# Sums of weight quadrants by accumulating loads, a full-height key low half, and a new order of the seven products

## The chip, the cores and the metric

One core of one Trainium2 chip. The metric is device microseconds of one execution. The kernel before took 1159.19 us (median of 3 runs, 1158.86 to 1163.72).

## The reference, cut to what matters

One hybrid decoder layer on 512 tokens with 16 meta tokens ahead (T = 528), width 2048, in fp32. A pre-RMSNorm, one input projection of 8192 columns, two groups of eight heads (stick-breaking attention with 128-wide heads; differential attention with two 64-wide query/key components, QK-norm and partial rotary), SiLU gates, one output projection of 2048 by 2048, and the residual:

```python
proj = jnp.einsum('btd,de->bte', rms_norm(h, norm_w), w_in)      # 2048 -> 8192
z = q @ k.T / sqrt(128); tail = reverse_cumsum(log_keep) - log_keep
a = where(k_pos < q_pos, exp(log_sigmoid(z) + tail), 0)           # stick-breaking head
p = softmax(where(k_pos <= q_pos, s, -inf))                       # for components 0 and 1
w = p[0] - lam * p[1]                                             # differential head
mixed = concat([sb_o * silu(sb_g), rms_norm(df_o, subln_w) * (1 - lam_init) * silu(df_g)])
out = h + mixed @ w_out
```

## The kernel before, in words

Every fp32 matrix product is done as three fp32r matmuls: each operand is split into a high part (a copy by ScalarE) and a low part (what is left, a subtraction by VectorE), and hi x hi, hi x lo, lo x hi are accumulated (`split`, lines 124 to 126; `mm`, lines 259 to 264).

The projections go by *pairs* of 128-column blocks: 32 pairs of w_in (numbers 0 to 31) and 8 of w_out (32 to 39). Four pairs belong to a head number: differential keys and values, differential queries and gate, stick-breaking keys and values, stick-breaking queries and gate. Pairs 2 to 31 and 33 to 39 use Strassen's scheme in Winograd's form: the weights of a pair are four quadrants a11, a21, a22, a12, the activations are seven combinations (`ut`), and seven products take the place of eight (`proj_pair`, line 431; `STEPS`, line 56). Each product is 8 (or 7) x 3 matmuls of 264 or 256 columns. The weights' side needs the sums s1 to s4. They are made by GpSimd in place on the raw quadrants (`SUMS`, `w_sum`, line 183), in two halves of 128x512 each, and each half is then split (`w_prep`, line 204). `preps` (line 218) runs through the pairs' quadrants in the order of use and goes one step on after each product. Raw quadrants have four places (tag "wr"), the split halves four each (tags "wh" and "wl"), so that splits are at most two quadrants ahead of TensorE: a split takes the place of the one two products back.

The products land in banks of PSUM (tag "pj", four). ScalarE copies those that are used more than once (`copied`, line 445), GpSimd adds copies (`add`, line 450), VectorE adds the last term from the bank (`final`, line 461). The pairs of w_out add onto the residual's rows (`base`).

Attention of a head runs beside the projections of the next pairs: `Pace` deals it out in steps. A differential head (`diff_head`) goes through four blocks of 128 queries and two components. Per block and component TensorE makes the scores (line 783 with the keys' high half, 785 the mask on the diagonal in bf16, 786 with the keys' low half on the component's 64 partitions), VectorE takes the row maximum (788, 789), ScalarE the exponential (791); then VectorE combines both components (797 to 799). Scores lie in two PSUM places, exponentials of component 0 in tag "w1" (two places), of component 1 in tag "w3" (one). `diff_k` prepares the keys: norm, rope, high and low half; the high half is copied to the other component's partitions too, since the query tile holds its high part on the component's 64 partitions and its low part on the other 64.

Loads go by SyncE's queue (line 157 for weights), in the order of the code. The order of instructions on each engine is laid out by a planner that plays the program through with its own durations; `hp(offset=600)` raises the priority of weight preparation and evictions. It is fixed before the run: an engine waits at an instruction whose input is late, with all that stands behind it.

Of the kernel before, what the change touches and what calls it, by code (L numbers as in the profile page):

```python
# [18 lines left out]
P = 128  # L19
# [64 lines left out]
def build(nc, tc, ctx, hT, win, wout, wpl, xT, prm, cst, out):  # L84
# [24 lines left out]
    def w3_tile(name, dt=F32):  # L109
        return ww.tile([P, T], dt, tag="w3", name=name, bufs=1)  # L110
# [29 lines left out]
    LOADS = ("a21", "a22", "a11", "a12")  # L140
# [8 lines left out]
    def w_load(s, which):  # L149
        o = s - last_in - 1  # L150
        if which == "pl":
            t = (cos_t, sin_t)[s % 2][:, :2 * NP * P].rearrange("p (k n) -> p k n", n=P)
            nc.sync.dma_start(t, wpl[o])
        else:
            t = wp.tile([P, H, P], F32, tag="wr", name=f"wr{s}{which}", bufs=4)[:, :depth(s)]
            if s > 0:
                nc.sync.dma_start(t, (win[s] if o < 0 else wout[o])[QUADS.index(which)])
        raw[s, which] = t

    def w_loads(s):  # L160
        order = QUADS if s in (1, 2, last_in + 2) else LOADS
        for which in () if s == len(plan) else order if s <= last_in else (*order, "pl"):
            w_load(s, which)

    def w_split(src, nm, spare=None):
# [3 lines left out]
        else:  # L169
# [5 lines left out]

    SUMS = {"s1": ("a21", "a21", "a22", ALU.add), "s2": ("a11", "a21", "a11", ALU.subtract),
            "s3": ("a21", "a22", "a11", ALU.subtract), "s4": ("a12", "a12", "a11", ALU.subtract)}

    def w_sum(s, which, u):
        if which in SUMS:  # L180
            o, x, y, op = SUMS[which]
            with hp(offset=600):
                G.tensor_tensor(raw[s, o][:, u], raw[s, x][:, u], raw[s, y][:, u], op=op)  # L183

    def w_halves(s, u, *which):

        v = units(s)[u]
        if s == 0:
            ts = [raw[s, x][:, v] for x in which]
        else:  # L190
            t = wp.tile([P, 2, 4, P], F32, tag="wr", name=f"wr{s}{which[0]}{u}", bufs=4)
            ts = [t[:, j, :v.stop - v.start] for j in range(2)]
# [11 lines left out]
    def w_prep(s, which, summed=False):  # L204

        for v in units(s):
            if which == "pl":
                v = slice(0, 2 * NP)
            elif not summed:
                w_sum(s, which, v)  # L210
            src = raw[s, SUMS[which][0] if which in SUMS else which]
            with hp(offset=600):
                wops.setdefault((s, which), []).append((v, *w_split(src[:, v], f"w{s}{which}{v.start}")))
            if which == "pl":
                break

    def preps():


        for s in range(1, len(plan)):  # L220
            if s == last_in + 1:
                continue
            while (s, "a12") not in raw:
# [8 lines left out]
            for which in [x for _, x, _ in STEPS2] if s == 2 else ("a11", "s1", "s2", "s3", "a12", "pl", "a22", "s4"):  # L232
                if which == "pl" and s <= last_in:
                    continue
                if s == 2 and which == "s3":
                    for v in units(s):
                        w_sum(s, "s2", v)
                w_prep(s, which, s == 2 and which == "s2")
# [9 lines left out]
    def combine(k, x, y, n, E, L=V):  # L248
# [3 lines left out]
        E.tensor_tensor(xs[:, 0], xs[:, 1], xs[:, 0], op=ALU.subtract)  # L252
        E.tensor_tensor(xs[:, 1], ys[:, 1], xs[:, 1], op=ALU.subtract)
        split(*(t[:, T1:T3 + 1] for t in hl), xs)
        E.tensor_tensor(ys[:, 1], ys[:, 1], xs[:, 0], op=ALU.subtract)
        E.tensor_tensor(ys[:, 0], ys[:, 0], ys[:, 1], op=ALU.subtract)
# [30 lines left out]
    for pool, tag, n in ((ww, "st", 5), (ww, "w1", 2), (ww, "w3", 1), (ww, "sh", 1), (sp, "vh", 1), (sp, "vl", 1)):  # L287
# [143 lines left out]
    def proj_pair(s, dst, base=None):  # L431
# [10 lines left out]
        def copied(x):  # L442
            t = wp.tile([P, TH], F32, tag="ev", name=f"ev{s}_{x}", bufs=4)[:, :n]
# [4 lines left out]
        def add(x, y):  # L448
            with hp(offset=600):
                G.tensor_tensor(x, x, y, op=ALU.add)  # L450

        def final(x, e, c, y):
            if (s, "pl") in wops:
                while late:
                    late.pop()()
                yield from plain(bank(x), e, c, wops[s, "pl"], x == "g")
            if base:
                y = base(e, c)
            with hp(offset=600):
                for d, sl in dst(e, c):  # L460
                    V.tensor_tensor(d, bank(x)[:, sl], y[:, sl], op=ALU.add)
# [3 lines left out]
        m1 = m5 = m7 = u2 = None  # L465
        for x, which, b in STEPS if s > 2 else STEPS2:
            more = which == "s2"
            yield from product(bank(x), wops[s, which], b, not more, x in "agd" or s <= last_in, more)
            next(ahead, None)
            if which == "a11":  # L470
                m1 = copied(x)
                if base:
                    add(base(0, 0), m1)
            elif which == "s1":
                m5 = copied(x)
            elif which == "s3":
                m7 = copied(x)
                if u2 is not None:
                    add(m7, u2)
                if base:  # L480
                    add(base(1, 0), m7)
            elif which == "s2":
                u2 = copied(x)
                add(m5, u2)
                if m7 is not None:
                    add(m7, u2)
                if base:
# [573 lines left out]
```

## Time and profile before

| | us | share of the span |
|---|---|---|
| profiled execution, its own time | 1159.92 | |
| its span | 1158.1 | |
| TensorE matmul busy | 1085.9 | 94% |
| VectorE busy | 958.3 | 83% |
| GpSimd busy | 793.9 | 69% |
| ScalarE busy | 612.7 | 53% |
| mean granted TensorE clock | 0.971 | |

Matmuls are pipelined: the duration of one (0.28 us for 256 columns) is longer than the distance from its start to the next one's start, and the distance is what counts on TensorE. A row of a timeline gives start, duration, engine, line, operation, tiles, shapes and count; in brackets the idle time before it and who ended it.

### The profile page before, as it was taken

To read this page: it belongs to the slowest core of one execution; us is meant where nothing else is said; L and a number is where in the kernel's file an instruction comes from. 1 tells how busy PE (TensorE), PEld (TensorE's weight loads), DVE (VectorE), ACT (ScalarE), POOL (GpSimd) and SP (SyncE) were. 2 spreads that over 40 slices of the span, in tenths; PEclk is the share of its full clock that TensorE was granted. 3 is DMA by queue.
4 is the path that set the end of the run, shared out by engine and by line. 5 is a ranking of instruction groups with operands and counts; after the bars stand their busy time and mean duration, and the time that the engine had idled before them with its cause. 6 is when DMAs were issued, how large, how long until landed. Compare 5 with 4: busy or idle time off the path is not lost.

```text
span 1158.1 us, 22082 instructions
## 1 busy us (share of the span) xinstructions
PE 1085.9 (94%) x8247; PEld 1022.0 (88%) x8247; DVE 958.3 (83%) x1556; ACT 612.7 (53%) x1231; POOL 793.9 (69%) x597
## 2 busy tenths in 40 slices
PE   8899999899989998999899999999999997799998
PEld 7898899799979997999799988998999886799998
DVE  6879887898788878887888789878887898978886
ACT  9735554455445544654465446544654565444443
POOL 3566668767866687668765877687657746658886
PEclk9999999999998999899989999999899988899999
DMA  7212222222222222222222222222222233345441
GB/s 273 78 53 74 73 83 83 73 74 83 83 73 74 82 83 74 73 83 83 73 74 83 83 74 73 83 83 73 74 82 83 92 94 112 112 155 158 150 139 68
DMA packets 37693, 106.39 MB, mean 92 GB/s; under 512 B 4433, under 2 KB 5713, under 8 KB 37585
## 3 DMA queue, kind: packets, MB, share of 16 engines
q1 hardware_dynamic: 37440, 104.96, 28.1%
q8 instruction: 65, 1.06, 0.4%
q14 instruction: 44, 0.35, 0.1%
q10 hardware_dynamic: 144, 0.01, 0.0%
HBM read 97.09 MB, written 7.86 MB: 91 GB/s over the span
## 4 chain that ended last, share of the span: by engine, by line
PE 47%; DVE 17%; POOL 14%; issue 13%; DMA 5%; ACT 4%; SPq 0%; DVEq 0%; ACTq 0%; POOLq 0%
POOL df_k_r L703 1%; PE df_s L786 1%; DVE sb_r L664 1%; POOL df_q_sh L687 1%; DVE utl L126 1%; PE df_o L608 1%; POOL df_k_sh L687 1%; PE df_s L783 1%; DVE df_p L798 1%; DVE a_all L666 1%; PE ps_ms L329 1%; DVE df_cf L797 1%; DVE df_qs L737 1%; DVE df_mx L789 1%; PE df_bc L716 1%
## 5 line engine op out<-in xcount | busy, mean ns | idle before, releaser
L791 ACT ACTIVATE df_p<-df_s,df_mx,df_q_r 128x144 f32<-128x144 f32 (+3 forms) x64 | 40.0, 626 | 45.5 <-DVE df_mx L789 45.4
L450 POOL TENSOR_TENSOR ev_g<-ev_g,ev_a 128x256 f32<-128x256 f32 (+1 forms) x37 | 40.5, 1094 | 28.8 <-ACT ev_g L445 28.8
L783 PE MATMUL df_s<-df_dk,df_qs 128*128 128x264 f32 (+3 forms) x80 | 30.6, 382 | 19.6 <-ACT df_p L791 17.6
L450 POOL TENSOR_TENSOR ev_d<-ev_d,ev_a 128x256 f32<-128x256 f32 (+1 forms) x37 | 42.8, 1156 | 3.3 <-ACT ev_a L445 3.3
L783 PEld LDWEIGHTS df_s<-df_dk,df_qs 128*128 128x128 f32 x80 | 16.4, 205 | 28.3 <-ACT df_p L791 21.7
L703 POOL TENSOR_TENSOR df_o_r<-df_o_m,mhalf 128x8 f32<-128x8 f32 x8 | 13.6, 1704 | 30.6 <-DVE df_o_m L699 30.6
L786 PE MATMUL df_s<-df_dk,df_qs 64*128 64x264 f32 (+3 forms) x80 | 34.5, 432 | 0.0
L664 DVE TENSOR_TENSOR_SCAN sb_r<-sb_k,ones 128x144 f32<-128x144 f32 (+3 forms) x32 | 31.1, 972 | 2.6 <-ACT sb_k L661 2.3
L788 DVE TENSOR_REDUCE df_mx<-df_s 128x1 f32<-128x144 f32 (+3 forms) x64 | 31.2, 496 | 1.0 <-PE df_s L786 1.0
L666 DVE TENSOR_TENSOR a_all<-sb_b,sb_r 128x143 f32<-128x143 f32 (+3 forms) x32 | 27.3, 854 | 2.3
L125 ACT ACTIVATE sb_ah<-sb_at 128x512 fp32r<-128x512 f32 (+4 forms) x40 | 16.6, 418 | 21.7 <-PE sb_at L587 20.8
L789 DVE TENSOR_TENSOR df_mx<-df_mx,df_q_r 128x1 f32<-128x1 f32 x64 | 25.9, 414 | 0.3
L703 POOL TENSOR_TENSOR df_k_r<-df_k_m,mhalf 128x10 f32<-128x10 f32 x8 | 18.9, 2365 | 9.7 <-DVE df_k_m L702 9.6
L661 ACT ACTIVATE sb_k<-sb_s,nrqs 128x144 f32<-128x144 f32 (+3 forms) x32 | 17.3, 541 | 14.8 <-PE sb_s L658 14.4
L662 ACT ACTIVATE sb_b<-sb_s,rqs 128x144 f32<-128x144 f32 (+3 forms) x32 | 17.2, 537 | 13.8 <-DVE a_all L666 13.8
L183 POOL TENSOR_TENSOR wr3a<-wr3a,wr3a 128x512 f32<-128x512 f32 x8 | 12.2, 1531 | 16.6 <-DMA wr3a<-in_win 8.2
L587 PE MATMUL sb_at<-ident,a_all 128*128 128x128 f32 x112 | 21.5, 286 | 1.8 <-DVE a_all L666 1.8
L786 PEld LDWEIGHTS df_s<-df_dk,df_qs 64*128 64x128 f32 x80 | 16.0, 200 | 7.4 <-issue 1.2
L587 PE MATMUL df_at<-ident,a_all 128*128 128x128 f32 x112 | 19.8, 274 | 2.1 <-DVE df_vl L126 2.1
L798 DVE TENSOR_SCALAR df_p<-df_p,df_rec 128x144 f32<-128x144 f32 (+3 forms) x32 | 21.8, 681 | 0.0
L125 ACT ACTIVATE df_ah<-df_at 128x512 fp32r<-128x512 f32 (+4 forms) x40 | 16.8, 420 | 8.2 <-PE df_at L587 6.8
L183 POOL TENSOR_TENSOR wr27a<-wr27a,wr27a 128x512 f32<-128x512 f32 x8 | 11.7, 1463 | 13.2 <-DVE w27a_l L126 9.3
(2775 smaller groups left out, 5791.0 us busy)
## 6 DMA issues: line engine op xcount, KB each, us to landing
xr<-in_xT SPq DMA_DIRECT2D x16, 256.0 KB, 2.7
out_dram<-xr SPq DMA_DIRECT2D x14, 256.0 KB, 2.2
wr0a<-in_win SPq DMA_DIRECT2D x8, 256.0 KB, 5.4
wr1a<-in_win SPq DMA_DIRECT2D x4, 512.0 KB, 5.2
wr2a<-in_win SPq DMA_DIRECT2D x4, 512.0 KB, 3.5
wr3a<-in_win SPq DMA_DIRECT2D x4, 512.0 KB, 4.1
wr4a<-in_win SPq DMA_DIRECT2D x4, 512.0 KB, 3.8
wr5a<-in_win SPq DMA_DIRECT2D x4, 512.0 KB, 3.8
```

Source lines behind the costliest of these rows:

```text
L125: S.activation(hi, src, AF.Copy)
L450: G.tensor_tensor(x, x, y, op=ALU.add)
L587: PE.transpose(pt[:kk, i * P:(i + 1) * P], a_t[i][:, b * P:b * P + kk], ident)
L664: V.tensor_tensor_scan(run[:, ::-1], keep[:, ::-1], ones_t.to_broadcast([P, n]), 1.0, op0=ALU.mult, op1=ALU.mult)
L666: V.tensor_tensor(a_t[i][:, :n - 1], beta[:, :n - 1], run[:, 1:], op=ALU.mult)
L703: G.tensor_tensor(r, m, mhalf[:, :2 * nb].rearrange("p (a c) -> p a c", c=2), op=ALU.pow)
L783: PE.matmul(o, qst[c][:, qs], dk[:, c, cs], start=True, stop=False)
L786: PE.matmul(o, qst[c][halves[c], qs], dk[halves[c], 2, cs], start=False, stop=True)
L788: V.tensor_reduce(mxn, view, axis=AX.XY if i == 3 else AX.X, op=ALU.max, negate=True)
L789: V.tensor_tensor(mxn, mxn, rqn[:, i, c:c + 1], op=ALU.mult)
L791: S.activation(sview(pt, i), view, AF.Exp, bias=mxn, scale=rqn[:, i, c:c + 1], accum_out=sums[:, c:c + 1])
L798: V.tensor_scalar(pts[0], pts[0], rec[:, 0:1], None, op0=ALU.mult)
```

## The change

Six things are changed together. (1) The sums of w_in's quadrants are no longer made by GpSimd. A second load of the other quadrant, issued from GpSimd, adds it to the raw quadrant in its place (`w_add`, `accum_op`); as only addition is used, signs of the sums and of the activations' combinations are turned, and with them those of the evictions. s1, s2 and s4 follow one another in a21's place, s3 lies in a11's. The adding load for s2 and that for s4 are issued behind the split of the sum before, that for s3 behind a11's split, that for s1 behind a21's load. w_out's sums stay on GpSimd. (2) The products come in the order a11, s1, a12, s2, a22, s3, s4 in all pairs, s3's product is added in the same bank as a11's and s2's, s2's bank is read once by VectorE, and GpSimd adds no copies except onto `base`. (3) The keys' low half is held for each component on all 128 partitions, and the third score matmul has 128 rows; the copies to the other 64 partitions are made by ScalarE. (4) Six raw places for quadrants instead of four, loads in the order a21, a11, a12, a22 (for w_out a11, a22, a21, a12). (5) Two places of tag "w3" instead of one. (6) The memory set aside for descriptors of GpSimd's DMAs is 2048 bytes instead of the default.

```diff
-STEPS = (("a", "a11", B11), ("d", "s1", T1), ("a", "s2", T2), ("g", "s3", T3),
-         ("b", "a12", B21), ("c", "a22", T4), ("e", "s4", B22))
-STEPS2 = tuple(STEPS[j] for j in (0, 4, 1, 3, 2, 5, 6))
+STEPS = (("a", "a11", B11), ("d", "s1", T1), ("b", "a12", B21), ("a", "s2", T2),
+         ("c", "a22", T4), ("a", "s3", T3), ("e", "s4", B22))
...
-        return ww.tile([P, T], dt, tag="w3", name=name, bufs=1)
+        return ww.tile([P, T], dt, tag="w3", name=name, bufs=2)
...
-    LOADS = ("a21", "a22", "a11", "a12")
+    LOADS = ("a21", "a11", "a12", "a22")
+    LOADS_OUT = ("a11", "a22", "a21", "a12")
...
-            t = wp.tile([P, H, P], F32, tag="wr", name=f"wr{s}{which}", bufs=4)[:, :depth(s)]
+            t = wp.tile([P, H, P], F32, tag="wr", name=f"wr{s}{which}", bufs=6)[:, :depth(s)]
...
+    SUMS = {"s1": ("a21", "a22"), "s2": ("a21", "a11"), "s4": ("a21", "a12"), "s3": ("a11", "a21")}
+    NEXT = {"s1": "s2", "s2": "s4", "a11": "s3"}
+    OUT_SUMS = {"s1": ("a21", "a21", "a22", ALU.add), "s2": ("a11", "a21", "a11", ALU.add),
+                "s3": ("a21", "a11", "a22", ALU.subtract), "s4": ("a12", "a12", "a11", ALU.add)}
+    def w_add(s, which):
+        place, more = SUMS[which]
+        nc.gpsimd.dma_start(raw[s, place], w_dram(s, more), accum_op=ALU.add)
     def w_loads(s):
...
             w_load(s, which)
+            if which == "a21" and 1 < s <= last_in:
+                w_add(s, "s1")
...
-    SUMS = {"s1": ("a21", "a21", "a22", ALU.add), "s2": ("a11", "a21", "a11", ALU.subtract),
-            "s3": ("a21", "a22", "a11", ALU.subtract), "s4": ("a12", "a12", "a11", ALU.subtract)}
-    def w_sum(s, which, u):
-        if which in SUMS:
-            o, x, y, op = SUMS[which]
-            with hp(offset=600):
-                G.tensor_tensor(raw[s, o][:, u], raw[s, x][:, u], raw[s, y][:, u], op=op)
...
+    def w_prep(s, which):
+        sums = SUMS if s <= last_in else OUT_SUMS
+        src = raw[s, sums[which][0] if which in sums else which]
+        for v in (slice(0, 2 * NP),) if which == "pl" else units(s):
+            if s > last_in and which in OUT_SUMS:
+                o, x, y, op = OUT_SUMS[which]
+                with hp(offset=600):
+                    G.tensor_tensor(raw[s, o][:, v], raw[s, x][:, v], raw[s, y][:, v], op=op)
             with hp(offset=600):
                 wops.setdefault((s, which), []).append((v, *w_split(src[:, v], f"w{s}{which}{v.start}")))
+        if s <= last_in and which in NEXT:
+            with hp(offset=600):
+                w_add(s, NEXT[which])
...
-            for which in [x for _, x, _ in STEPS2] if s == 2 else ("a11", "s1", "s2", "s3", "a12", "pl", "a22", "s4"):
+            for which in ("a11", "s1", "a12", "pl", "s2", "a22", "s3", "s4"):
...
-        for x, which, b in STEPS if s > 2 else STEPS2:
-            more = which == "s2"
+        for x, which, b in STEPS:
+            more = which in ("s2", "s3")
...
             elif which == "s1":
-                m5 = copied(x)
-            elif which == "s3":
-                m7 = copied(x)
-                if u2 is not None:
-                    add(m7, u2)
-                if base:
-                    add(base(1, 0), m7)
-            elif which == "s2":
-                u2 = copied(x)
-                add(m5, u2)
-                if m7 is not None:
-                    add(m7, u2)
-                if base:
-                    add(base(0, 1), m5)
-                    add(base(1, 1), m5)
-            else:
-                yield from final(x, *{"b": (0, 0, m1), "e": (0, 1, m5), "c": (1, 0, m7)}[x])
-        yield from final("g", 1, 1, m5)
+                m5 = copied(x, "d")
+                onto_base(1, 1, m5)
+            elif which == "a12":
+                yield from final(x, 0, 0, m1)
+            elif which == "s2":
+                u4 = ev("u")
+                with hp(offset=600):
+                    V.tensor_tensor(u4, bank(x), m5, op=ALU.add)
+                onto_base(0, 1, u4, ALU.subtract)
+            elif which == "s3":
+                u3 = copied(x, "g")
+                onto_base(1, 0, u3, ALU.subtract)
+                yield from final("c", 1, 0, u3, ALU.subtract)
+                yield from final(x, 1, 1, m5)
+            elif which == "s4":
+                yield from final(x, 0, 1, u4, ALU.subtract)
...
-        dk = sp.tile([P, 3, T], F32R, tag="sdk", name=nm + "_dk")
-        tl = dk[:, 2]
+        dk = sp.tile([P, 4, T], F32R, tag="sdk", name=nm + "_dk")
         for c in range(2):
-            th, h = dk[:, c], halves[c]
+            th, tl, h, o = dk[:, c], dk[:, 2 + c], halves[c], halves[1 - c]
             S.activation(th[h], k[h], AF.Copy)
             V.tensor_tensor(tl[h], k[h], th[h].bitcast(F32), op=ALU.subtract)
-            V.tensor_copy(th[halves[1 - c]], th[h].bitcast(F32))
+            S.activation(th[o], k[h], AF.Copy)
+            S.activation(tl[o], tl[h].bitcast(F32), AF.Copy)
...
-                    PE.matmul(o, qst[c][halves[c], qs], dk[halves[c], 2, cs], start=False, stop=True)
+                    PE.matmul(o, qst[c][:, qs], dk[:, 2 + c, cs], start=False, stop=True)
...
-    nc = bacc.Bacc("TRN2", target_bir_lowering=False, num_devices=1)
+    nc = bacc.Bacc("TRN2", target_bir_lowering=False, num_devices=1,
+                   dynamic_dma_scratch_size=2048)
```

## Rows read from the trace of the kernel before

**Rows 1.** The page: busy us (share of the span) and instructions of each engine.

```profile
PE 1085.9 (94%) x8247; PEld 1022.0 (88%) x8247; DVE 958.3 (83%) x1556; ACT 612.7 (53%) x1231; POOL 793.9 (69%) x597
```

**Rows 2.** Waits: who waited for whom, us in total, times, longest us.

```profile
ACT df_p L791 <- DVE df_mx L789: 45.4, 19, 4.8
...
PE df_s L783 <- ACT df_p L791: 17.6, 16, 1.4
```

**Rows 3.** Stretch 452 to 463 us: busy of PE, PEld, DVE, ACT, POOL; timeline.

```profile
452.00:463.00 11.00, 9.49 (x64) 7.91 (x63) 10.90 (x20) 4.82 (x12) 8.40 (x7) 1.00 0.14 48
...
453.20 0.69 DVE L126 TENSOR_TENSOR w15a_l<-wr15a,w15a_h 128x512 fp32r<-128x512 f32 x1
...
454.29 1.57 DVE L126 TENSOR_TENSOR w15a_l<-wr15a,w15a_h 128x512 fp32r<-128x512 f32 x1
...
454.02 1.28 POOL L183 TENSOR_TENSOR wr15a<-wr15a,wr15a 128x512 f32<-128x512 f32 x1 [1.16 <-DVE df_mx L789]
...
455.60 0.63 ACT L125 ACTIVATE w15s_h<-wr15a 128x512 fp32r<-128x512 f32 x1 [0.28 <-PE pj14e L264]
```

**Rows 4.** Timeline of PE at the last block's first scores of a differential head.

```profile
461.88 0.39 PE L783 MATMUL df_s<-df_dk,df_qs 128*128 128x264 f32 x1 [1.39 <-ACT df_p L791]
462.20 0.38 PE L786 MATMUL df_s<-df_dk,df_qs 64*128 64x264 f32 x1
462.51 0.39 PE L783 MATMUL df_s<-df_dk,df_qs 128*128 128x264 f32 x1
```

**Rows 5.** Windows at half clock and one after; behind POOL the clock.

```profile
344.27:354.51 10.24, 10.24 (x41) 8.88 (x41) 7.38 (x17) 5.79 (x13) 2.02 (x2) 0.50 0.06 10
463.74:470.57 6.83, 6.83 (x29) 5.92 (x29) 5.55 (x12) 4.45 (x10) 0.80 (x1) 0.50 0.00 0
470.57:479.40 8.83, 8.83 (x77) 8.81 (x77) 7.13 (x11) 6.60 (x13) 6.86 (x5) 1.00 0.35 117
...
931.37:938.19 6.82, 6.82 (x29) 5.91 (x28) 6.35 (x14) 4.68 (x11) 0.88 (x1) 0.50 0.00 0
```

**Rows 6.** Timeline of PE: a differential score of 272 columns and what follows.

```profile
448.81 0.29 PE L783 MATMUL df_s<-df_dk,df_qs 128*128 128x272 f32 x1
...
449.10 0.39 PE L786 MATMUL df_s<-df_dk,df_qs 64*128 64x272 f32 x1
449.42 0.39 PE L263 MATMUL pj14c<-utl,w14a_h 128*128 128x264 f32 x1
449.64 0.29 PE L264 MATMUL pj14c<-uth,w14a_l 128*128 128x264 f32 x1
```

**Rows 7.** Timeline of PE: a stick-breaking score of 264 columns with diagonal.

```profile
392.73 0.28 PE L654 MATMUL sb_s<-sb_sk,sb_q 128*128 128x264 f32 x1
...
393.10 0.28 PE L658 MATMUL sb_s<-sb_sk,sb_q 128*128 128x264 f32 x1
393.22 0.29 PE L262 MATMUL pj12c<-uth,w12a_h 128*128 128x264 f32 x1
```

**Rows 8.** Groups by line: count, busy us, mean ns, idle before.

```profile
L450 POOL TENSOR_TENSOR ev_d<-ev_d,ev_a 128x256 f32<-128x256 f32 (+1 forms) x37 | 42.8, 1156 | 3.3 <-ACT ev_a L445 3.3
...
L183 POOL TENSOR_TENSOR wr14a<-wr14a,wr14a 128x512 f32<-128x512 f32 x8 | 12.9, 1628 | 4.2 <-DVE w14a_l L126 2.2 <-DMA wr14a<-in_win 1.3 <-POOL o13b L555 0.7
```

**Rows 9.** DMA: queue (packets, MB, share); issues (count, KB, us to landing).

```profile
q1 hardware_dynamic: 37440, 104.96, 28.1%
...
xr<-in_xT SPq DMA_DIRECT2D x16, 256.0 KB, 2.7
...
wr13a<-in_win SPq DMA_DIRECT2D x4, 512.0 KB, 3.7
```

**Rows 10.** Timeline: s1's last split and the fourth product's start, pairs 13 and 14.

```profile
401.98 1.17 DVE L126 TENSOR_TENSOR w13s_l<-wr13a,w13s_h 128x512 fp32r<-128x512 f32 x1
...
411.46 0.28 PE L262 MATMUL pj13g<-uth,w13s_h 128*128 128x256 f32 x1
...
430.58 1.45 DVE L126 TENSOR_TENSOR w14s_l<-wr14a,w14s_h 128x512 fp32r<-128x512 f32 x1
...
437.60 0.28 PE L262 MATMUL pj14g<-uth,w14s_h 128*128 128x264 f32 x1
```

More of the change, by code (lines that the diff above doesn't have):

```diff
@@ L154, in w_load, with w_dram @@
         else:
[L155 removed]
+            t = wp.tile([P, H, P], F32, tag="wr", name=f"wr{s}{which}", bufs=6)[:, :depth(s)]
             if s > 0:
[L157 removed]
+                nc.sync.dma_start(t, w_dram(s, which))
         raw[s, which] = t
+    def w_dram(s, which):
+        o = s - last_in - 1
+        return (win[s] if o < 0 else wout[o])[QUADS.index(which)]
+    SUMS = {"s1": ("a21", "a22"), "s2": ("a21", "a11"), "s4": ("a21", "a12"), "s3": ("a11", "a21")}
[5 more added lines that the diff above has]
+        nc.gpsimd.dma_start(raw[s, place], w_dram(s, more), accum_op=ALU.add)
     def w_loads(s):
[L161 to L162 removed]
+        order = QUADS if s == 1 else LOADS
+        for which in () if s == len(plan) else order if s <= last_in else (*LOADS_OUT, "pl"):
             w_load(s, which)
+            if which == "a21" and 1 < s <= last_in:
+                w_add(s, "s1")
     def w_split(src, nm, spare=None):
@@ L190, in w_halves @@
         else:
-            t = wp.tile([P, 2, 4, P], F32, tag="wr", name=f"wr{s}{which[0]}{u}", bufs=4)
+            t = wp.tile([P, 2, 4, P], F32, tag="wr", name=f"wr{s}{which[0]}{u}", bufs=6)
             ts = [t[:, j, :v.stop - v.start] for j in range(2)]
@@ L222, in preps @@
                 continue
-            while (s, "a12") not in raw:
+            while (s, "a22") not in raw or (s, "a12") not in raw:
                 yield
@@ L231, in preps @@
                 continue
-            for which in [x for _, x, _ in STEPS2] if s == 2 else ("a11", "s1", "s2", "s3", "a12", "pl", "a22", "s4"):
+            for which in ("a11", "s1", "a12", "pl", "s2", "a22", "s3", "s4"):
                 if which == "pl" and s <= last_in:
                     continue
[L235 to L238, printed above, removed]
+                w_prep(s, which)
                 yield
@@ L446, in copied, with onto_base, final @@
             return t
[L448 to L452, printed above, removed]
+        def onto_base(e, c, x, op=ALU.add):
+            if base:
+                with hp(offset=600):
+                    G.tensor_tensor(base(e, c), base(e, c), x, op=op)
+        def final(x, e, c, y, op=ALU.add):
             if (s, "pl") in wops:
@@ L455, in final @@
                     late.pop()()
-                yield from plain(bank(x), e, c, wops[s, "pl"], x == "g")
+                yield from plain(bank(x), e, c, wops[s, "pl"], x == "a")
             if base:
-                y = base(e, c)
+                y, op = base(e, c), ALU.add
             with hp(offset=600):
                 for d, sl in dst(e, c):
-                    V.tensor_tensor(d, bank(x)[:, sl], y[:, sl], op=ALU.add)
+                    V.tensor_tensor(d, bank(x)[:, sl], y[:, sl], op=op)
@@ L463, in proj_pair @@
         if s != last_in:
             w_loads(s + 1)
-        m1 = m5 = m7 = u2 = None
-        for x, which, b in STEPS if s > 2 else STEPS2:
-            more = which == "s2"
-            yield from product(bank(x), wops[s, which], b, not more, x in "agd" or s <= last_in, more)
+        for x, which, b in STEPS:
+            more = which in ("s2", "s3")
+            yield from product(bank(x), wops[s, which], b, not more, x in "ad" or s <= last_in, more)
             next(ahead, None)
             if which == "a11":
-                m1 = copied(x)
-                if base:
-                    add(base(0, 0), m1)
+                m1 = copied(x, "a")
+                onto_base(0, 0, m1)
@@ L528, in second_pair @@
                 for d, sl in dst(e, 1):
-                    V.tensor_tensor(d, banks[e][1][:, sl], m[e], op=ALU.add)
+                    V.tensor_tensor(d, banks[e][1][:, sl], m[e], op=ALU.subtract)
     at_off = [0, 256, 640, 1152]
```

27 lines of the change are left out of this document (10 added, 17 removed).

## The prediction

> **What bounds the kernel now.** I read five things in this order: the busy shares, the waits, the windows around the longest TensorE wait, the timeline of each engine there, and the DMA issues. The busy shares [rows 1] show TensorE at 94% and VectorE at 83%, with GpSimd at 69%. So every column that TensorE streams, and every stall of it, counts in full, while other engines' work counts only where TensorE waits for it. The waits [rows 2] show where that is: the largest wait of TensorE in total, 17.6 us in 16 pieces, is a differential score (line 783) waiting for the exponential of an earlier block (line 791), and the exponential in turn waited 45.4 us for the row maximum on VectorE (line 789). In the window around one such wait [rows 3] VectorE is busy 10.90 of 11.00 us: inside a differential head VectorE is the local bound. Part of its work there is slowness, not work: the same subtraction (128x512, line 126) takes 0.69 us where GpSimd is idle and 1.57 us where a sum of w_in starts on GpSimd 0.27 us earlier [rows 3]. Right after the score that waited 1.39 us [rows 4] the granted clock is at 0.50 (1.2 of 2.4 GHz) for 6.8 us [rows 5]. Five such stretches lie in the heads, the first of 10.24 us and the last of 6.82; these and three like them between are 41 us in all.
>
> **The change, part by part.**
>
> *Keys' low halves on all partitions.* The third score matmul had 64 rows, the others 128. From a 272-column 128-row score through the diagonal and the 64-row matmul and one projection matmul, to the start of the next one, it takes 449.64 - 448.81 = 0.83 us [rows 6]. The stick-breaking chain with the same count of instructions (score, diagonal, two more of 264 columns) takes 393.22 - 392.73 = 0.49 us [rows 7]. The 64-row one alone starts 0.32 us ahead of what follows it, against 0.12 for a 128-row one. So 0.34 us each, for 64 score groups with a diagonal (8 heads, 4 blocks, 2 components): 21.8 us. The 16 spans without a diagonal go from 462.51 - 461.88 = 0.63 us [rows 4] to 2 x 0.12 = 0.24 us: 6.2 us. Sum 28; I take 25, because some of these matmuls stand next to a wait that would swallow the gain. Bounds: 0 if something other than the row count makes the pitch, and 28. The price: two more ScalarE copies per component and head (32 of 64x528) and one cast less on VectorE. Neither engine is where keys are waited for (they are made a pair ahead), ScalarE is the least busy, so I count nothing; uncovered, it would be 32 copies at the 0.63 us of a 128x512 one [rows 3], 20 us of ScalarE, and of the path only what a key is then late.
>
> By the Trainium skill (TensorE: Matmul & The Clock Gate, section LDWEIGHTS) a weight load of few partitions takes as long as one of 128, and its section Why this matters for your kernels says that a matmul of small K takes the time of K=128; by that this edit would be worth nothing. The rows differ: 0.32 us against 0.12. A sum by the rule would lack these 25 us; it is a rival below.
>
> *Sums of w_in off GpSimd.* Four sums in two halves for 30 pairs are 240 operations of about 1.6 us [rows 8], some 380 us of GpSimd. None is on TensorE's path by itself. What goes with them is the slowing of VectorE: 0.9 us per collision [rows 3]. In the 11 us window GpSimd is busy 8.40 us [rows 3], about four of its seven operations being sums; without them VectorE gets some 3 to 4 us back there, more than the 1.39 us that the score waited. I take two thirds of the 17.6 us [rows 2], 12 us, as gained; bounds 0 (the order of the engines' work is laid out anew and may put the same wait elsewhere) and 17.6. With the wait the half clock should go in part. In it 29 matmuls run in 6.83 us, in the stretch after it 77 in 8.83 us [rows 5]: half the time of the 41 us is lost, 20 us. I take 10; bounds 0 and 20.
>
> *The sums as accumulating loads.* 120 transfers of 512 KB, which no row of the trace shows. Traffic: 105 MB take 28.1% of the DMA engines [rows 9]; 63 MB more read from HBM, and as much read back from SBUF, add about 34% at the same share per MB: 62%, not the bound. Latency: a plain 512 KB load lands 3.7 us after its issue and one of 256 KB 2.7 us [rows 9], so each further 256 KB costs about 1 us. Two streams give 3.7 + 2 = 5.7 us, my value; bounds 3.7 (as a plain load) and 11.1 (read, read and write one after another). What it has to fit into: the sum for s2 can be issued only when s1's low half has been read, and is wanted when the fourth product starts, less one split (a copy of 0.63 us and a subtraction of 0.69 [rows 3], 1.3 us). In the pair of stick-breaking keys, s1's split ends at 430.58 + 1.45 = 432.03 and the fourth product starts at 437.60 [rows 10]: 5.6 us, so 4.3 for the transfer. In the next kind of pair it is 411.46 - 403.15 = 8.3 [rows 10], 7.0 for the transfer; the other pairs lie about there or above. At 5.7 us only the seven or so pairs of the first kind are late, by 1.4 us less the time VectorE wins (1.45 us instead of 0.69 in that very split): I charge 6 us, bounds 0 and the rival below. The later sum (s4, from s2's split to the seventh product) has three products of time between, and s3 needs only a11's split. On GpSimd an issue that waits holds back what is queued behind it: the rope products, the gates, the power of line 703 that the key scale waits for. GpSimd will be some 40% free, so I count nothing for that; it is part of the 6.
>
> The Trainium skill (SBUF — State Buffer, section SBUF: two separate sides) says that the descriptors of a DMA issued from GpSimd can't be written while VectorE holds the shared ports in a two-port operation, so that such a DMA seems blocked by VectorE. No row here shows one. It speaks against this change, with VectorE busy 99% in the window above; its result is the third rival.
>
> *New evictions.* s2's ScalarE copy and two GpSimd additions (line 450, 1.16 us each [rows 8], 37 pairs) become one VectorE operation that reads the bank, about as long as 0.7 us at most [rows 3]; 37 of them, 26 us at the very most, against far more that VectorE gets back. Five banks per pair instead of six, in four buffers; no wait for a bank is among TensorE's large ones [rows 2]. Nothing counted, and likewise for the second buffer under the second component's exponential: ScalarE waited for the maximum, not for a buffer [rows 2].
>
> *Two raw places more, new load order, smaller scratch, pair 2 in the common order.* SyncE's loads now wait less; nothing waits for them among TensorE's waits. Nothing, within 3 us either way (the start of pair 2 is the one place where loads come late).
>
> *Sum.* The profiled execution took 1159.9 us (span 1158.1 and 1.8 around it), 0.7 above the median shown. 1159.9 - 25 - 12 - 10 + 6 = 1118.9; less the 0.7, 1118 us.
>
> **The rivals.**
>
> First, the row count buys nothing and the rest holds: 1118 + 25 = 1143 us. For it: the diagonal ahead is bf16, and the change of type costs too. Against it: the spans without a diagonal show the same 0.3 us [rows 4]. 8%.
>
> Second, only the row count counts: the waits and the half clock stay, since the new order of work puts another wait in the place, or issuing the loads keeps GpSimd as busy with VectorE as the sums did. 1159 - 25 + 6 = 1140 us. For it: the score waits recur at the same two blocks of each head, a property of the order. Against it: VectorE full in that window. 20%.
>
> Third, the other side: the accumulating loads come late. Place: the split of s2 on ScalarE and VectorE, with everything queued behind it, then TensorE's fourth product, and again at s4. Price: each microsecond beyond the room costs one per pair, 30 us. Room is 7.0 us in the common pair, and the gains of 47 us cover 1.6 us more, so it decides from about 8.6 us to landing. At 9.5 us it gives 1159 - 47 + 30 x 2.5 = 1187 us, at the upper bound of 11.1 some 1235. For it: no row shows such a load, and the chain s1, s2, s4 goes through one place in SBUF. Against it: 5.7 us by streams, and TensorE has attention work to put in. 17%.
>
> Between the second and third lies a loss that cancels the gain (a landing about 8.6 us): 5%, within the bound below.
>
> **How the numbers follow.** The forecast of 1118 us has 50%, the rivals 8, 20 and 17%, the cancelling 5%. About 0.5% (6 us) is what can be told from no change here. Faster: 50 + 8 + 20 less 1 for a weak case, 77%; the same 6%; slower 17%. The forecast's own range is 1102 to 1134: below, the wait and the clock at their better ends (5.6 and 10 us less); above, the wait's 12 us lost and 4 more for late pairs. The range reaches below to the better ends of all terms but one, 1159 - 28 - 17 - 20 = 1094, say 1096, and above over both faster rivals and the cancelling case to 1164; out of it lie most of the slow rival and a few per cent below.
>
> **What would show it.** Right: the line of the low-half score starts about 0.12 us ahead of its follower; the wait of line 783 for line 791 falls under 8 us; subtractions of the splits at 0.69 us nearly throughout; fewer half-clock stretches in the heads; accumulating loads landing in under 7 us. Wrong: waits of ScalarE's w copies on such loads, repeated in every pair, or GpSimd standing at an issue while line 703 or a gate is queued behind it.

## The result, and the profile after

The changed kernel takes 1110.57 us (median of 4 runs, 1107.7 to 1111.3), the one before 1159.74 us beside it: a ratio of 0.9565, with a 95% interval of 0.9537 to 0.9593. That is faster by 49 us, where 42 were forecast, and inside the range. The profiled execution took 1107.7 us.

The page's first line, after:

```profile
PE 1043.3 (94%) x8247; PEld 999.6 (90%) x8247; DVE 827.4 (75%) x1577; ACT 618.7 (56%) x1226; POOL 438.5 (40%) x403
```

Beside [rows 1], VectorE fell by 131 us with 21 more instructions, and GpSimd by 355 us. TensorE's share stayed at 94%, so it still has 62.6 us in which it does nothing. The mean granted clock rose from 0.971 to 0.986.

TensorE at a differential score of 272 columns with diagonal (start, duration, instruction), to be read beside [rows 6]:

```profile
428.77 0.29 PE L790 MATMUL df_s<-df_dk,df_qs 128*128 128x272 f32 x1
428.90 0.23 PE L792 MATMUL df_s<-mdf,idb 128*128 128x128 bf16 x1
428.94 0.37 PE L793 MATMUL df_s<-df_dk,df_qs 128*128 128x272 f32 x1
429.15 0.28 PE L269 MATMUL pj14a<-utl,w14s_h 128*128 128x264 f32 x1
429.27 0.28 PE L270 MATMUL pj14a<-uth,w14s_l 128*128 128x264 f32 x1
```

From the score to the second start behind the low-half matmul it is 0.50 us where it was 0.83. Start by start: 0.17 from the score to the low half (0.29 before), 0.21 from there to the follower (0.32), and 0.12 to the next (0.22). The 0.12 that the prediction named as its sign is reached only by the 16 low halves without a diagonal ahead; the bf16 diagonal keeps the other 64 at 0.21 in the median.

Where the time went shows in the weight loads (PEld). These are the loads of the low half and of its follower before, and of the follower after:

```profile
449.10 0.18 PEld L786 LDWEIGHTS df_s<-df_dk,df_qs 64*128 64x128 f32 x1
449.41 0.19 PEld L263 LDWEIGHTS pj14c<-utl,w14a_h 128*128 128x128 f32 x1
...
429.02 0.19 PEld L269 LDWEIGHTS pj14a<-utl,w14s_h 128*128 128x128 f32 x1
```

In a stream of 128-row matmuls a load starts 0.12 us ahead of its matmul (the median of some 8000); after, the follower's load is 0.13 us ahead. Before, all 80 loads of 64 rows and all 80 that follow one start with their matmul, at most 0.002 us ahead. No two 64-row matmuls stand one behind the other, so whether the 64 rows or the change of row count does it can't be told.

The waits after (who waited for whom, us in total, times, longest), in place of [rows 2]:

```profile
ACT df_p L798 <- DVE df_mx L796: 31.6, 18, 2.4
...
PE sb_o L614 <- ACT sb_ah L123: 8.7, 7, 1.3
...
ACT w30s_h L123 <- DMA wr30a<-in_win: 6.3, 1, 6.3
...
ACT w14s_h L123 <- DMA wr14a<-in_win: 5.3, 1, 5.3
...
PE df_s L790 <- ACT df_p L798: 3.1, 7, 0.5
```

The score's wait fell from 17.6 to 3.1 us. New are ScalarE's waits for the adding loads, in nearly every pair, 109.6 us together. TensorE's waits for the products of s2 and s3 are only 16.1 us in the list of waits, so most of ScalarE's waiting does not show there as a wait of TensorE for a weight. For 8.7 us TensorE waits for the attention copy sb_ah, which ScalarE makes; an experiment below shows that this wait does not come from the adding loads' lateness.

One of the waits for an adding load, followed through the engines (pair 14; bracket: idle before and what ended it):

```profile
410.79 0.67 DVE L124 TENSOR_TENSOR w14s_l<-wr14a,w14s_h 128x512 fp32r<-128x512 f32 x1
...
411.83 0.88 POOL L173 DMA_DIRECT2D wr14a<-in_win  x1 [1.85 <-DVE w14s_l L124]
...
418.78 1.15 ACT L123 ACTIVATE w14s_h<-wr14a 128x512 fp32r<-128x512 f32 x2 [5.26 <-DMA wr14a<-in_win]
419.84 0.37 ACT L454 ACTIVATE ev_d<-pj14d 128x264 f32<-128x264 f32 x1
...
419.46 0.39 PE L268 MATMUL pj14a<-uth,w14s_h 128*128 128x264 f32 x1 [0.16 <-ACT w14s_h L123]
```

VectorE reads s1 last until 411.46; the adding load is issued at 411.83, and its sum is read 6.95 us later. Read the brackets against each other: TensorE waited 0.16 us, ScalarE 5.26 us. Behind ScalarE's copy stood the eviction of bank d, and further down its queue the copies that the next head's first scores need.

The DMA issues (KB each, median us from issue to landing) and queues, beside [rows 9]:

```profile
q0 software_dynamic: 17280, 62.92, 33.0%
q1 hardware_dynamic: 37440, 104.96, 29.1%
...
wr13a<-in_win SPq DMA_DIRECT2D x4, 512.0 KB, 4.4
wr13a<-in_win POOLq DMA_DIRECT2D x4, 512.0 KB, 6.2
...
wr14a<-in_win POOLq DMA_DIRECT2D x4, 512.0 KB, 7.2
```

Adding loads land after 5.5 to 8.2 us by pair (median of all 120: 5.7, the estimate; of the 30 for s2: 5.5), and plain loads beside them after 3.4 to 4.8.

### The profile page after: what moved, and what is told of

Read it like the earlier page. It is cut to its first block, busy times and chain, and to the rows that moved or that the text cites. A ratio compares the mean times of both kernels' runs of the same rounds, so it can differ in the third digit from the quotient of the medians.

```text
span 1105.9 us, 21873 instructions
## 1 busy us (share of the span) xinstructions
PE 1043.3 (94%) x8247; PEld 999.6 (90%) x8247; DVE 827.4 (75%) x1577; ACT 618.7 (56%) x1226; POOL 438.5 (40%) x403
## 3 DMA queue, kind: packets, MB, share of 16 engines
q0 software_dynamic: 17280, 62.92, 33.0%
q1 hardware_dynamic: 37440, 104.96, 29.1%
## 4 chain that ended last, share of the span: by engine, by line
PE 63%; DVE 12%; DMA 10%; ACT 7%; issue 5%; POOL 2%; ACTq 0%; DVEq 0%; POOLq 0%; SPq 0%
PE sb_o L614 2%; PE df_o L614 2%; DVE utl L124 1%; ACT df_p L798 1%; DVE df_mx L795 1%; PE sb_at L593 1%; DVE df_qs L743 1%; PE df_bc L722 1%; PE df_km L757 1%; DMA wr30a<-in_win 1%; PE df_at L593 1%; ACT L563 1%; DMA wr6a<-in_win 1%; PE df_om L825 1%; DVE utl L332 1%
## 5 line engine op out<-in xcount | busy, mean ns | idle before, releaser
L793 PE MATMUL df_s<-df_dk,df_qs 128*128 128x264 f32 (+3 forms) x80 | 29.1, 363 | 0.0
L790 PE MATMUL df_s<-df_dk,df_qs 128*128 128x264 f32 (+3 forms) x80 | 25.0, 321 | 4.2 <-ACT df_p L798 3.1
L672 DVE TENSOR_TENSOR a_all<-sb_b,sb_r 128x143 f32<-128x143 f32 (+3 forms) x32 | 20.9, 653 | 2.4
L124 DVE TENSOR_TENSOR df_al<-df_at,df_ah 128x512 fp32r<-128x512 f32 (+4 forms) x40 | 18.9, 475 | 4.2 <-ACT df_ah L123 3.5
L614 PE MATMUL sb_o<-sb_ah,sb_vh 128*128 128x512 f32 (+4 forms) x35 | 13.1, 375 | 8.7 <-ACT sb_ah L123 8.7
L124 DVE TENSOR_TENSOR sb_al<-sb_at,sb_ah 128x512 fp32r<-128x512 f32 (+4 forms) x40 | 18.7, 470 | 2.1 <-ACT sb_ah L123 2.1
L593 PEld LDWEIGHTS sb_at<-ident,a_all 128*128 128x128 f32 x112 | 13.1, 137 | 5.9 <-DVE a_all L672 4.7
L806 DVE SCALAR_TENSOR_TENSOR a_all<-df_p,df_cf,df_p 128x144 f32<-128x144 f32 (+3 forms) x32 | 17.9, 559 | 0.0
L268 PE MATMUL pj<-uth,w32a_h 128*128 128x256 f32 x56 | 16.4, 318 | 1.2 <-ACT w32a_h L123 0.7
L270 PE MATMUL pj<-uth,w32a_l 128*128 128x256 f32 x56 | 16.9, 310 | 0.0
```

The lines of the kernel that those rows point to most:

```text
L124: E.tensor_tensor(lo, src, hi.bitcast(F32), op=ALU.subtract)
L593: PE.transpose(pt[:kk, i * P:(i + 1) * P], a_t[i][:, b * P:b * P + kk], ident)
L614: PE.matmul(po[:, qs], x[:kk, b], y[:kk], start=(b == 0 and n_ == 0), stop=(b == NKB - 1 and n_ == 2))
L672: V.tensor_tensor(a_t[i][:, :n - 1], beta[:, :n - 1], run[:, 1:], op=ALU.mult)
L790: PE.matmul(o, qst[c][:, qs], dk[:, c, cs], start=True, stop=False)
L793: PE.matmul(o, qst[c][:, qs], dk[:, 2 + c, cs], start=False, stop=True)
```

## The experiments

Ratios are to the kernel before, run beside each, with 95% intervals. What is worked out between two experiments goes by their ratios times 1160 us.

**Only the row count, in the kernel before.**

```diff
-        dk = sp.tile([P, 3, T], F32R, tag="sdk", name=nm + "_dk")
-        tl = dk[:, 2]
+        dk = sp.tile([P, 4, T], F32R, tag="sdk", name=nm + "_dk")
...
-                    PE.matmul(o, qst[c][halves[c], qs], dk[halves[c], 2, cs], start=False, stop=True)
+                    PE.matmul(o, qst[c][:, qs], dk[:, 2 + c, cs], start=False, stop=True)
```

> The kernel before with the keys' full-height low half alone (and the 2048-byte scratch, so that it fits). If the row count is worth what the pitches say, 25 us: 1135 us, the low-half score 0.12 us ahead of its follower, and the wait of the score for the exponential still near 17 us. If the row count buys nothing (the rival), 1159 us.

1159.65 us, 0.9981 [0.9961, 1.0001]: 2 us, and not told from none, instead of 25. Its waits:

```profile
ACT df_p L791 <- DVE df_mx L789: 55.7, 24, 5.1
...
PE df_s L783 <- ACT df_p L791: 26.8, 24, 1.7
```

TensorE is busy 1056.8 us instead of 1085.9, but the score's wait grew from 17.6 to 26.8 us and that of the exponential from 45.4 to 55.7 [rows 2]: faster scores arrive at a VectorE that is no faster. The time at half clock fell all the same, from 68 to 44 us (mean granted clock 0.971 to 0.982), and brought no time with it.

**Only the row count undone, in the changed kernel** (the reverse edit).

> The changed kernel with the 64-row low half put back. By the row count as a term of its own: 1110.6 + 25 = 1135 us. If the row count and the relief of VectorE overlap (part of both is the same wait and half clock in the heads), less: 1120 to 1128. If the row count buys nothing, 1110.

1110.31 us, 0.9562 [0.9527, 0.9598]: no loss. ScalarE's waits for adding loads shrink from 109.6 to 91.9 us; TensorE's longer time filled them.

**The sums back on GpSimd, the rest kept** (loads in the order that such sums want).

```diff
-        for which in () if s == len(plan) else order if s <= last_in else (*LOADS_OUT, "pl"):
+        for which in () if s == len(plan) else LOADS_OUT if 1 < s <= last_in else order if s <= last_in else (*LOADS_OUT, "pl"):
             w_load(s, which)
-            if which == "a21" and 1 < s <= last_in:
-                w_add(s, "s1")
...
-        sums = SUMS if s <= last_in else OUT_SUMS
+        sums = OUT_SUMS
...
-            if s > last_in and which in OUT_SUMS:
+            if which in OUT_SUMS:
...
-        if s <= last_in and which in NEXT:
-            with hp(offset=600):
-                w_add(s, NEXT[which])
```

> The changed kernel with w_in's sums made by GpSimd again, as w_out's are, and w_in's quadrants loaded in w_out's order; new order of products, six places, full-height keys stay. If GpSimd's sums slow VectorE and with it the heads: 1125 to 1140 us, splits' subtractions back near 0.9 us in the mean, half clock in the heads again. If the new order and the places bring the gain beside the row count, 1105 to 1112.

1139.81 us, 0.9815 [0.9778, 0.9852]. Its score wait is back where [rows 2] had it, and VectorE's busy time is 978.9 us:

```profile
ACT df_p L793 <- DVE df_mx L791: 65.3, 32, 4.5
...
PE df_s L785 <- ACT df_p L793: 19.9, 15, 2.4
```

So the adding loads win 29 us net, and the rest of the change some 21. The sums as such are not late here: ScalarE waits 3.6 us in all for w_in's sums by GpSimd.

**No adding loads at all** (both calls of `w_add` removed).

> The changed kernel with the 120 adding loads left out (the products s1 to s4 of w_in then take unsummed quadrants). What they cost by their lateness: 6 us as charged gives 1104 us; the stalls that the trace of after shows at the s2 and s4 products, some 25 us, give 1085; if the loads cost nothing on the path, 1110.

1053.52 us, 0.9071 [0.9039, 0.9103]:

```profile
PE 1024.0 (97%) x8247; PEld 995.1 (95%) x8247; DVE 820.1 (78%) x1577; ACT 628.2 (60%) x1226; POOL 341.7 (33%) x283
```

Less than each of the three times expected. Same 8247 matmuls, 97% busy: here TensorE is the bound. The adding loads therefore cost 57 us, where 6 were charged, and what they replace was worth 86 (0.9815 to 0.9071).

Where the loads cost TensorE time can be counted from the start of each matmul to the next one's, in this trace and in that of the changed kernel (spans 1051.1 and 1105.9 us, 55 apart). Ahead of s2's matmuls stand 9 us more in the pairs of stick-breaking keys and 16 more in those of stick-breaking queries, and nothing more in the other two kinds of pair; 9 more stand ahead of scores, 9 ahead of the product that waits for sb_ah, and 5 ahead of a22's. So about half is the late weight itself.

**The same with 64 rows** (the former and the row count undone).

> The kernel without adding loads (s1 to s4 of w_in unsummed), with the 64-row low half put back. There TensorE is 97% busy and waits for nothing in the heads. If the row count is worth its pitch only where TensorE is the bound: 1053 + 20 to 25 = 1073 to 1078 us. If it is worth nothing anywhere, 1053.

1080.16 us, 0.9300 [0.9274, 0.9326]. The row count is worth 26.6 us as soon as TensorE is the bound: 0.33 us for each of 80 matmuls, close to the 28 worked out. With 64 rows the adding loads cost 30 us, with 128 rows 57, and both end at 1110: in the changed kernel the adding loads bind, and the room that they leave swallows what TensorE saves.

**s2's load issued twice** (the sum then holds a11 twice).

```diff
-                w_add(s, NEXT[which])
+                for _ in range(2 if which == "s1" else 1):
+                    w_add(s, NEXT[which])
```

> The changed kernel with the adding load for s2 issued twice, one behind the other (the sum then holds a11 twice). It lands some 6 us later in each of 30 pairs. If lateness has its full price once the room is used up, as the third rival had it, 30 x 6 = 180 us: about 1290 us. If TensorE's other work fills part of the wait, 1170 to 1230; if the adding loads had room left, under 1130.

1236.25 us, 1.0666 [1.0612, 1.0721]: 128 us for 30 loads, 4.3 us each, where the second load lands 5.8 us behind the first (median).

```profile
PE pj6a L269 <- ACT w6s_h L123: 6.0, 1, 6.0
...
PE pj14a L269 <- ACT w14s_h L123: 5.0, 1, 5.0
```

TensorE now waits for s2 itself, 124.5 us in 31. That is 22 us for each microsecond of lateness, where the third rival's price was 30. Part of it is clock: TensorE's idle time grows by 92 us, and the rest of the 126 us between the two profiled executions is longer busy time, with 160 us at half clock instead of 34.

**Loads in halves, each behind its half's split.**

```diff
-    def w_add(s, which):
+    def w_add(s, which, v=slice(0, H)):
...
-        nc.gpsimd.dma_start(raw[s, place], w_dram(s, more), accum_op=ALU.add)
+        nc.gpsimd.dma_start(raw[s, place][:, v], w_dram(s, more)[:, v], accum_op=ALU.add)
...
-        if s <= last_in and which in NEXT:
-            with hp(offset=600):
-                w_add(s, NEXT[which])
+                if s <= last_in and which in NEXT:
+                    w_add(s, NEXT[which], v)
```

> The changed kernel with the adding loads for s2, s3 and s4 issued in two halves, each right behind the split of its half. If what the loads cost is that they land late for the next split (ScalarE waits 115 us for them in all, about 4 us per pair), a half issued about 1.5 us earlier and landing about 1.5 us sooner takes some two thirds of it away: 1075 to 1095 us. If the cost is the issue on GpSimd or the traffic, 210 issues instead of 120 make it slower: 1112 to 1125.

1085.34 us, 0.9351 [0.9315, 0.9387]: 25 us less with 210 issues instead of 120 and the same bytes. So neither the number of issues nor the traffic is the main cost; ScalarE's waits for adding loads fall to 61.8 us.

**a22's product ahead of s2's** (splits likewise).

```diff
-STEPS = (("a", "a11", B11), ("d", "s1", T1), ("b", "a12", B21), ("a", "s2", T2),
-         ("c", "a22", T4), ("a", "s3", T3), ("e", "s4", B22))
+STEPS = (("a", "a11", B11), ("d", "s1", T1), ("b", "a12", B21), ("c", "a22", T4),
+         ("a", "s2", T2), ("a", "s3", T3), ("e", "s4", B22))
```

> The changed kernel with the product of a22 moved ahead of that of s2 (and its split likewise), so that the adding load for s2 has one product, about 4 us, more. If lateness is the cost, most of the 57 us that leaving the loads out brought come back: 1062 to 1080 us, ScalarE's waits for adding loads under 40 us in all. If issue and traffic are the cost, 1110.

1166.04 us, 1.0039 [1.0013, 1.0065]: outside what was expected, 55 us slower than the changed kernel with the same loads. Pair 15:

```profile
474.04 0.88 POOL L173 DMA_DIRECT2D wr15a<-in_win  x1 [1.04 <-DVE w15s_l L124]
...
479.71 1.15 ACT L123 ACTIVATE w15s_h<-wr15a 128x512 fp32r<-128x512 f32 x2 [3.50 <-DMA wr15a<-in_win]
...
480.39 0.58 PE L268 MATMUL pj15e<-uth,w15s_h 128*128 128x256 f32 x1 [3.16 <-ACT w15s_h L123]
```

A product more ahead of s2 is one fewer between s2 and s4. The wait moved to s4's split, where the pair has no other product left: TensorE waits 53.4 us there, in the changed kernel 0, although ScalarE's waits for adding loads fell to 64.7 us. The granted clock falls to 0.960. What a wait costs depends on what TensorE has left at that place.

**Halves and a22 first.**

> Halves and a22 first together. If lateness is the cost and either change alone leaves a rest of it, 1055 to 1065 us, close to the 1053 without any adding load; if a22 first alone already gives enough room, the same as that run within 4 us, or a little slower for the further issues.

1079.97 us, 0.9309 [0.9284, 0.9334], slower than expected. With halves the same order wins 5 us (the two intervals overlap) where it lost 55.

**Halves, and s1's product first** (order s1, a11, a12, s2, a22, s3, s4, for the splits likewise).

```diff
-STEPS = (("a", "a11", B11), ("d", "s1", T1), ("b", "a12", B21), ("a", "s2", T2),
+STEPS = (("d", "s1", T1), ("a", "a11", B11), ("b", "a12", B21), ("a", "s2", T2),
```

> Adding loads in halves, and s1 as the first product (s1, a11, a12, s2, a22, s3, s4), so that s2's sum has a product more of room and s4's keeps the two that it has. If lateness of the chain s1, s2, s4 is what is left: 1060 to 1075 us, under the 1080 of halves with a22 first and the 1085 of halves alone. If the wait only moves on to s4 again, 1080 to 1090.

1069.68 us, 0.9207 [0.9178, 0.9236], which beats both kernels: one product more between s1 and s2 and as many as before behind s2. ScalarE's waits for adding loads are down to 8 us, and TensorE is at 96%:

```profile
PE 1026.1 (96%) x8247; PEld 995.7 (93%) x8247; DVE 839.5 (79%) x1577; ACT 625.2 (59%) x1226; POOL 515.0 (48%) x493
```

The wait for sb_ah is as long as in the changed kernel, though hardly any adding load is late here:

```profile
PE sb_o L613 <- ACT sb_ah L123: 8.7, 7, 1.3
```

**GpSimd's sums with the former places.** The third experiment with four raw places and one "w3":

```diff
-        return ww.tile([P, T], dt, tag="w3", name=name, bufs=2)
+        return ww.tile([P, T], dt, tag="w3", name=name, bufs=1)
...
-            t = wp.tile([P, H, P], F32, tag="wr", name=f"wr{s}{which}", bufs=6)[:, :depth(s)]
+            t = wp.tile([P, H, P], F32, tag="wr", name=f"wr{s}{which}", bufs=4)[:, :depth(s)]
```

> The kernel with GpSimd's sums in the new order (1139.8 us), with four raw places and one place of the second exponential as before. If the 20 us by which that kernel beats the one before come from the order of the products and the fewer evictions (74 additions on GpSimd less): 1137 to 1143 us. If the places bring them: 1150 to 1160.

1170.34 us, 1.0077 [1.0048, 1.0105], more than either time expected. The new order of products, evictions and loads with the row count is by itself 9 us slower than before. GpSimd waits 190.9 us for raw quadrants (44.7 in the kernel before), for instance:

```profile
POOL wr25a L217 <- DMA wr25a<-in_win: 9.8, 1, 9.8
...
PE df_o L609 <- POOL df_ah L597: 11.3, 7, 2.5
```

Pair 14's first load is issued 14 us before the pair's first product, and while a sum waits for its load, whatever is queued behind it on GpSimd waits too: line 597 is a memset of 0.2 us, and TensorE waits 11.3 us for it, which is not among the waits of the next experiment.

**The same with six raw places and one "w3".**

> The kernel with GpSimd's sums in the new order (1139.8 us), with one place of the second exponential as before, and the six raw places kept. If that one place makes most of the 30 us that both kinds of places were worth: 1158 to 1170 us, with ScalarE's exponentials waiting some 70 us for row maxima as with both undone. If the raw places make them: 1138 to 1146.

1137.33 us, 0.9803 [0.9768, 0.9838]. The two raw places are worth 32 us (1.0077 to 0.9803): pair 14's first load goes out 40 us ahead, and GpSimd's waits for loads fall to 71 us. The second "w3" place is worth nothing (0.9803 and 0.9815 lie in each other's intervals).

## Why the prediction was right

The direction was right, and so was the mechanism of the gain: sums off GpSimd relieve VectorE, and the loads that replace them take part of it back by landing late. That the time came within 8 us of the forecast was luck: four terms of the sum were mis-sized and made each other good, and the prediction's own sign of being wrong, ScalarE's copies waiting for such loads in every pair, stands in the trace. The steps between the experiments, by their ratios:

| step | predicted us | measured us |
|---|---|---|
| new order, evictions and loads, with the row count, former places | 0 for the order | +9 |
| six raw places | 0 | -32 |
| second "w3" place | 0 | +1 (within the intervals) |
| sums off GpSimd, and with it what the row count is worth | -47 | -86 |
| adding loads late | +6 | +57 |
| sum | -41 | -51 |

The experiments did not all run beside one another, and the worth of a step depends on what is already there.

*Row count, -25.* The pitch is as predicted: 0.33 us per group saved (0.83 in [rows 6], 0.50 after), and 26.6 us where TensorE is the bound. As time it gave 2 us in the kernel before and nothing in the changed one, so the first rival was right that it buys nothing there, for another reason. Its point for itself, the bf16 diagonal, costs 0.09 us per group (0.21 against 0.12). The bound of 0 was put down to the row count not making the pitch; it came from the next wait in line, VectorE's maximum before and the adding loads after. By the Trainium skill (TensorE: Matmul & The Clock Gate, section Why this matters for your kernels) a single matmul of small K takes as long as one of K=128. In this mix with 128-row matmuls the runs differ: 1080.16 against 1053.52 us.

*Relief of VectorE, -12 and -10.* The signs came as listed: score wait 17.6 to 3.1 us; of the 420 subtractions of w_in's splits (128x512) 374 take under 0.75 us instead of 249, the mean is 773 ns instead of 968; clock 0.971 to 0.986. The clock is no sign of the relief, though, since the row count alone had brought 0.982 and no time; no run shows its 10 us by themselves. The size was too small. Of the 86 us some 25 are the row count coming into effect, if it is worth as little beside GpSimd's sums in the new order as in the kernel before (2 us; not run there), and some 60 are left for the relief, against 22 predicted and 38 as the sum of its bounds. That they are relief, and not sums that were late, is what the waits of the third and fourth experiments say: of ScalarE for VectorE 217 us with the sums on GpSimd and 71 without any, of TensorE for VectorE 40 and 11, of ScalarE for the sums 3.6. The bounds were taken from one wait and the half clock; they left out most of what VectorE loses beside GpSimd. It is held rather than slowed: a two-input operation that starts during one of GpSimd ends with it or right behind it.

```profile
451.05 1.82 POOL L183 TENSOR_TENSOR wr15a<-wr15a,wr15a 128x512 f32<-128x512 f32 x1
...
451.62 1.26 DVE L789 TENSOR_TENSOR df_mx<-df_mx,df_q_r 128x1 f32<-128x1 f32 x1
```

The sum ends at 452.87 and the maximum at 452.88; alone such a maximum takes 0.15 us. Counted against the quickest quarter of the same operation and shape, VectorE lost 231 us before, in 356 operations that each overlap one of GpSimd, and 106 after, which is nearly all of the 131 us by which its busy time fell. The short operations of the softmax chain lose most for their size. Groups of VectorE, before (count, busy us, mean ns, idle before):

```profile
L789 DVE TENSOR_TENSOR df_mx<-df_mx,df_q_r 128x1 f32<-128x1 f32 x64 | 25.9, 414 | 0.3
...
L797 DVE TENSOR_TENSOR df_cf<-df_rec,ones 128x1 f32<-128x1 f32 x32 | 19.6, 613 | 1.1
```

and after:

```profile
L796 DVE TENSOR_TENSOR df_mx<-df_mx,df_q_r 128x1 f32<-128x1 f32 x64 | 10.0, 161 | 0.2
...
L804 DVE TENSOR_TENSOR df_cf<-df_rec,ones 128x1 f32<-128x1 f32 x32 | 8.0, 249 | 1.1
```

*Adding loads, +6.* This is the step that failed. The landing time was right (a median of 5.7 us for the estimate of 5.7), and so was the traffic (33.0% for an estimate of 34%). That "only the seven or so pairs of the first kind are late" was wrong. Those pairs, of stick-breaking keys, cost 9 us at s2's product, near the 6 charged. The pairs of stick-breaking queries cost 16, some 2 us each: the stretch from s1's last split to the fourth product [rows 10] was taken from the former order, where "the other pairs lie about there or above" 8.3 us, but without adding loads it is 6.7 us in them (6.7 to 10.2 over pairs 3 to 31). In these pairs s2's load is issued 1.1 us behind s1's split and lands 5.5 us later, and TensorE starts 0.8 us behind that (medians), 7.4 in all, so 0.7 of the 2 us are accounted for. The rest of the 57 us came at other places. ScalarE waits in every kind of pair, some 4 us a pair, because its copy stands in its queue as soon as its turn comes, and evictions and the head's copies stand behind it. The third rival described this, "with everything queued behind it", but put its start at a landing of 8.6 us. The doubled load shows the price, and the halves and the s1-first order show that it is mainly lateness and not issue or traffic.

*Places, nothing.* Failed for the six raw places: the prediction looked for waits of TensorE on loads. The waits were GpSimd's, 190.9 us of them with the former places, and what TensorE saw of them had another name (line 597). In the kernel as changed the worth of the places was not tried.

*Descriptors blocked by VectorE.* No sign of it: each of GpSimd's issues takes 0.85 to 1.2 us and the loads land as two streams would. The Trainium skill (SBUF — State Buffer, section SBUF: two separate sides) lets one fear a stall there while VectorE runs a two-port operation; at VectorE's 75% none is seen, and the trace does not tell which of its operations are such.

What stays open: whether the 9 us ahead of scores go through ScalarE's queue was not tried by a run. Nor was it tried why the best version stays 16 us above the one without adding loads. TensorE has two waits there that the other does not have, 8.7 us for sb_ah and 4.6 us for a22's low half; the cause of the first is not known, and the further issues on GpSimd and the traffic were not tried alone.

## What to carry to other kernels

A pitch gained on an engine counts only where no other wait is next; look for that wait before charging the gain, and test it by taking the other wait away. A late input costs at the engine that bounds the kernel and also in the in-order queue where its consumer stands, with everything behind it; look at both, and in every kind of pair in the new order. How early a load could start was decided here by free places, and two of them were worth about as much, in the kernel with GpSimd's sums, as the row count's whole gain.

## What the runs showed of the hardware

- Adding loads took 33.0% of the DMA engines' time for 62.92 MB where plain ones took 29.1% for 104.96 MB: 1.9 times as much per MB. Where no other sum's load stood close by, an adding load of half the size landed sooner: the first half of s4's after 4.1 us and the second after 4.9 (medians of 30 pairs, loads in halves), the whole one after 5.5. With halves of three sums close together little is gained (7.0 us instead of 7.2 in pair 14, with halves and a22 first).
- A two-input VectorE operation that starts while GpSimd runs a two-input operation was held until that one ended. In the trace before, 54 one-column operations began with over 0.2 us of such a GpSimd operation left, and all 54 ended 0.01 to 0.02 us after it; of 221 weight splits in that place 204 ended 0.5 to 0.65 us after it. So the mean of the one-column maximum is 414 ns before and 161 ns after, and most of them take 0.15 us in both. It is not w_in's sums alone: with a22 first, where GpSimd makes none of those, the mean is 373 ns, and other operations of GpSimd (lines 546 and 644) stand in their place.
- A weight load started 0.12 us ahead of its matmul in a stream of 128-row matmuls, and with it at each of the 160 changes between 128 and 64 rows; 80 low halves of 64 rows cost 26.6 us where TensorE was the bound.
